# Lending the ring of split weight pairs to expert weights in a two-block model kernel

## Chip, cores and metric

The kernel runs on one core of one Trainium2 chip. Its time is the device time of one execution in microseconds (us), given as the median of several runs. Engine names: PE is TensorE, PEld its weight loads, DVE is VectorE, ACT is ScalarE, POOL is GpSimd, SP is SyncE, whose queue issues nearly all transfers here.

## What is computed

Two blocks follow each other on 256 tokens of width 1024, all in float32. Block 1 is a mixer (pooling and differential attention, closed by the dense product with `w_out`) and then a layer of 32 experts, of which each token takes two. Block 2 is a state-space layer (SSM), a latent-attention layer (MLA) and a last norm. The part around the change, cut to its core:

```python
x = x + (gate_p * pool_out + gate_a * attn_out) @ w_out[l]        # last dense product of block 1
hn = rmsnorm(x, norm2_g[l]).reshape(B * S, D)
x = x + hier_moe(hn, ...)                                          # router, then 32 experts:
#   hdn = silu(xb @ w_gate[e]) * (xb @ w_up[e]);  y = (hdn @ w_down[e]) * wb
...
u = rms_norm(h, norm_w[0])                                         # block 2, first layer
y = ssd_mixer(u, ...)                                              # begins with u @ ssm_in_w
```

The weights of the 32 experts are 32 x 3 x 2 MB = 192 MB. All of them are loaded, whatever the router chooses.

## The kernel before

**Weights come as one list.** `specs` holds every weight piece in the order of use, each 8 KB per partition or less (1 MB in all for a full one). `Weights.issue` (L64) takes the next piece of the list, allots a tile `raw` in some pool, and has SP issue one transfer into it (L77). Pieces of dense layers are worked on further; pieces of experts (192 of them, step `None`) are read by PE as they are.

**Dense pieces are split.** PE works here on pairs of reduced-precision float32 tiles. `_split` (L81) takes 1024 columns of a raw piece: ACT copies them, rounded, into `whi`, and DVE subtracts to get the remainder `wlo` (both L92). Each of the two tiles is 4 KB per partition, and the pool `chp` keeps four of each (`CH_BUFS`): this is the ring of split pairs, 32 KB per partition in all. A product then takes three matmuls per pair: `whi` with the high part of the input, then two more, in `mm3` (L401 to L404) or, as a generator that lets other work in between, `mm3s` (L408). Where the weights are PE's stationary operand (`gemm_feat`, `fine_feat`), the last of the three reads `wlo`; where they are the moving one (`gemm_tok`, `last_out`), it reads `whi`. Splits run ahead of their use by three pairs (five in block 2, where two more pairs live in another pool, `W.more`).

**Where expert weights may lie.** Raw tiles come from four pools: `rawp` (3 slots, L213), `raw2` (7, L778), `raw3` (5, L808) and `raw4` (1, L969), 16 slots of 8 KB. The last three open one after the other as block 1 frees its space. When PE has used a piece, `W.done` (L125) issues the next piece of the list into the pool just freed; with `until=expert_end` these three pools take no piece behind the experts, so the first pieces of the SSM layer go to `rawp` alone. SP issues in the order of the program, and a transfer waits on SP until its slot is free; each also reuses one of eight semaphores, so at most eight are under way.

**The stage between.** The last dense product takes the last four pairs at once (`cs = W.take(4)`, L928) and works through `last_out`; its last use of `whi` are two extra matmuls (`WARM3`, L954). Then come the router (`place`, L856) and the first gather (`gather0`, L917), and then the eight rounds of experts, four experts each: `gate_up` (L1033, matmuls L1043), `hidden_T`, `down` (L1062, matmuls L1069), with the gather of the next round and the scatter of the last one woven in. A round uses 24 pieces. During the eight rounds no pair is split: `W.stop` holds the splits back until L1124, behind the last round.

**Order.** A scheduler places the instructions of each engine when the program is built; a few `order(...)` calls pin pairs of them. So a change of a tile's size or of what it waits for can move instructions elsewhere in the program.

Of the kernel before, what the change touches and what calls it, by code (L numbers as in the profile page):

```python
# [10 lines left out]
F32R = mybir.dt.float32r  # L11
# [7 lines left out]
P = 128  # L19
# [7 lines left out]
CH_BUFS = 4  # L27
MORE = 2
CH = 1024
# [3 lines left out]
HOLD1 = 4  # L33
HOLD2 = 3
ATT = 0.08


class Weights:


    def __init__(self, tc, raw_pool, ch_pool, specs):
        self.tc, self.nc = tc, tc.nc
        self.raw_pool, self.ch_pool = raw_pool, ch_pool
        self.specs = specs
        self.raw = {}
        self.issued = 0
        self.chunks = []
        self.stop = None
        for i, (ap, a, b, step) in enumerate(specs):
            if step is None:  # L50
                self.stop = len(self.chunks)
                continue
            for a0 in range(0, a, step):
                self.chunks.append((i, a0, min(step, a - a0), b, a0 + step >= a))
        self.split = 0
        self.next_whole = None
        self.ready = {}
        self.used = 0
        self.behind = ()
        self.more = None  # L60
        self.between = lambda: None
        self.limit = CH_BUFS + MORE
# [18 lines left out]
    def _split(self):  # L81
        nc = self.nc
        c = self.split
        i, a0, n, b, last = self.chunks[c]
        v = self.raw[i][0][:, a0:a0 + n, :]
        pool = self.more if self.more is not None and c % (CH_BUFS + MORE) >= CH_BUFS else self.ch_pool
        bufs = CH_BUFS if pool is self.ch_pool else MORE
        hi = pool.tile([P, CH], F32R, name="whi", tag="whi", bufs=bufs)
        lo = pool.tile([P, CH], F32R, name="wlo", tag="wlo", bufs=bufs)
        hv = hi[:, :n * b].rearrange("p (a b) -> p a b", b=b)  # L90
        lv = lo[:, :n * b].rearrange("p (a b) -> p a b", b=b)
        pair = self.last = (nc.scalar.copy(hv, v), nc.vector.tensor_sub(lv, v, hv.bitcast(F32)))  # L92
        for later, earlier in zip(pair, self.behind):
            if earlier is not None:
                order(self.tc, later, earlier)
        self.ready[c] = (hv, lv)
        if last:
            _, pool, until = self.raw.pop(i)
            self.issue(pool, until)
        self.split += 1  # L100
# [48 lines left out]
def order(tc, later, earlier):  # L149

    tc.add_manual_dep(later.ins, earlier.ins.name,
                      mybir.DependencyInfo(mybir.DependencyClass.NoSync, mybir.DependencyReason.DATA), reason="order")
# [50 lines left out]
def model_kernel(ctx: ExitStack, tc: tile.TileContext, ap, out, taps=None, stop=None):  # L203
# [10 lines left out]
    ch_pool = ctx.enter_context(tc.tile_pool(name="chp", bufs=CH_BUFS))  # L214
# [23 lines left out]
    for e4 in range(0, 32, 4):  # L238
        for name, step in (("w_expert_gate", 2), ("w_expert_up", 2), ("w_expert_down", 1)):
            kt, n = ap[name].shape[2] // P, ap[name].shape[3]  # L240
# [5 lines left out]
    expert_end = len(specs)  # L246
# [14 lines left out]
    W = Weights(tc, raw_pool, ch_pool, specs)  # L261
# [260 lines left out]
    with b1:  # L522
# [7 lines left out]
        hl = wx.tile([P, 8, T], F32R, name="hl", tag="hl")  # L530
# [303 lines left out]
        def x_part(t, k0, n, add):  # L834

            c = slice(k0 * P, (k0 + n) * P)
            nc.vector.tensor_add(x_sb[:, t, c], x_sb[:, t, c], add)
            sq, sc = rt.tile([P, 512], F32, name="sq")[:, :n * P], ss[:, t, k0 // 2:k0 // 2 + 1]
            if k0 < 6:
                square_sum(x_sb[:, t, c], sq, sc)  # L840
            else:
                nc.vector.tensor_tensor_reduce(sq, x_sb[:, t, c], x_sb[:, t, c], 1.0, 0.0, OP.mult, OP.add, sc)
            if k0 == 0:
                lt[t] = mp.tile([P, 512], F32, name="m")
            ps = mp.tile([P, 4, P], F32, name="m")
            for k in range(n):
                nc.tensor.transpose(ps[:, k], x_sb[:, t, (k0 + k) * P:(k0 + k + 1) * P], ident)
            xT = rt.tile([P, 4, P], F32, name="xT", bufs=2)
            act = nc.scalar.copy(xT[:, :n], ps[:, :n])
            for k in range(k0, k0 + n):  # L850
                pe = nc.tensor.matmul(lt[t][:, :40], xT[:, k - k0], wr[:, k], start=(k == 0), stop=(k == 7))
            return act, pe
# [90 lines left out]
        act, _ = x_part(0, 4, 4, po[0])  # L943
# [16 lines left out]
    with ExitStack() as b2:  # L960
# [3 lines left out]
        yp = b2.enter_context(tc.tile_pool(name="exy", bufs=2, space=PSUM, reuse_waits="tile"))  # L964

        rt_.close()
        x2_sb = ctx.enter_context(tc.tile_pool(name="x2p", bufs=1, reuse_waits="tile")).tile([P, 2, D], F32, name="x2_sb")
        raw4_ = ExitStack()
        raw4 = raw4_.enter_context(tc.tile_pool(name="raw4", bufs=1, reuse_waits="tile"))  # L969
# [437 lines left out]
    with ExitStack() as b4:  # L1407
# [206 lines left out]
        def rest(share):  # L1614

            while share >= ATT * done[0]:
                done[0] += 1
# [161 lines left out]
```

## Time and profile before

| what | value |
|---|---|
| median of 3 runs | 1102.57 us (1102.52 to 1104.97) |
| the profiled execution, its own time | 1104.54 us |
| its span in the trace | 1102.9 us |
| PE, DVE, ACT busy, share of the span | 90%, 45%, 36% |
| moved by the transfers | 293.64 MB, mean 266 GB/s |

The profile shows one execution. Busy shares are means over stages with different limits, so the share of PE says little by itself: a stage is read from its stretch of time, with the rate of the transfers (GB/s) beside the busy time of the engines. A wait is named by the engine and line that waited, and by what ended the wait last. Where the line is that of a helper (L77, L92, L404, L408), it stands for every call of that helper, so the stretch has to tell which one it is.

### The profile page before, as it was taken

The numbers are of one execution on the slowest core, as the hardware profiler recorded it, in microseconds if no ns is written. First come the engines' busy times: TensorE is split into PE (matmuls) and PEld (weight loads), VectorE is DVE, ScalarE is ACT, GpSimd is POOL, SyncE is SP. The second block draws the span as 40 slices with busy tenths as digits, with TensorE's granted clock in tenths as the row PEclk, the third lists the DMA queues.
The fourth block names the chain that finished last, engine by engine and source line by source line (L and its number), as shares of the span: only waits on it lengthen the run. The fifth ranks groups of instructions, "written<-read, shape, count | busy, mean of one in ns | idle before, by whom it ended". The sixth has DMA issues, their size and how long they took to land. (4 is left out here: it accounts for less than half of the span.)

```text
span 1102.9 us, 14835 instructions
## 1 busy us (share of the span) xinstructions
PE 987.2 (90%) x5981; PEld 688.6 (62%) x5981; DVE 492.0 (45%) x1085; ACT 394.1 (36%) x740; POOL 0.2 (0%) x4
## 2 busy tenths in 40 slices
PE   8999998996979687887967679999999999999997
PEld 6899986441414131231411139899998879999985
DVE  8587565120202010100100037679687576467764
ACT  5456542000000000000000036884855555476652
POOL 0000000000000000000000000000000000000000
PEclk9999998999989899989999999999999999999999
DMA  8444895999999999999999966244335446444331
GB/s 297 153 154 153 292 409 187 409 408 410 408 409 409 409 409 409 409 409 410 409 409 409 409 236 229 94 175 140 128 116 177 150 136 219 134 136 123 116 111 39
DMA packets 97096, 293.64 MB, mean 266 GB/s; under 512 B 6912, under 2 KB 12032, under 8 KB 97024
## 3 DMA queue, kind: packets, MB, share of 16 engines
q1 hardware_dynamic: 96736, 292.13, 70.5%
q8 instruction: 48, 0.79, 0.3%
q10 hardware_dynamic: 288, 0.52, 0.1%
q14 instruction: 24, 0.20, 0.1%
HBM read 291.58 MB, written 1.05 MB: 265 GB/s over the span
## 5 line engine op out<-in xcount | busy, mean ns | idle before, releaser
L92 DVE TENSOR_TENSOR wlo<-raw,whi 128x1024 fp32r<-128x1024 f32 (+2 forms) x175 | 202.8, 1170 | 92.4 <-ACT whi L92 91.0
L92 ACT CAST whi<-raw 128x1024 fp32r<-128x1024 f32 (+2 forms) x175 | 175.6, 1011 | 152.8 <-PE acc L403 52.7
L1043 PE MATMUL ea<-raw,xg 128*32 128x512 f32 x1024 | 173.6, 640 | 55.5 <-DMA raw<-in_w_expert_up_dram 50.1
L1043 PEld LDWEIGHTS ea<-raw,xg 128*32 128x32 f32 x1024 | 34.7, 112 | 171.5 <-DMA raw<-in_w_expert_up_dram 100.5
L1069 PE MATMUL yps<-raw,hT 128*32 128x512 f32 x512 | 103.6, 598 | 30.9 <-DMA raw<-in_w_expert_down_dram 25.5
L408 PE MATMUL acc<-u,whi 128*128 128x256 f32 x512 | 96.7, 286 | 0.0
L1069 PEld LDWEIGHTS yps<-raw,hT 128*32 128x32 f32 x512 | 21.9, 109 | 107.0 <-DMA raw<-in_w_expert_down_dram 63.6
L1052 DVE TENSOR_TENSOR hx<-sg,ea 128x512 f32<-128x512 f32 x8 | 5.5, 688 | 185.0 <-PE ea L1043 185.0
L1084 DVE TENSOR_TENSOR x_sb<-x_sb,m 128x512 f32<-128x512 f32 x32 | 22.0, 687 | 144.4 <-PE m L1083 144.4
L408 PEld LDWEIGHTS acc<-u,whi 128*128 128x128 f32 x512 | 79.9, 189 | 1.5
L408 PE MATMUL acc<-u,wlo 128*128 128x256 f32 x256 | 73.2, 286 | 0.0
L908 PEld LDWEIGHTS m<-Sr,x_sb 128*128 128x128 f32 x224 | 55.0, 334 | 8.8 <-issue 8.1
L1060 ACT COPY hT<-m 128x512 f32<-128x512 f32 x8 | 4.7, 586 | 152.9 <-PE m L1058 152.9
L908 PE MATMUL m<-Sr,x_sb 128*128 128x128 f32 x224 | 55.8, 402 | 0.0
L402 PE MATMUL acc<-hh,whi 128*128 128x256 f32 x192 | 55.8, 291 | 0.0
L404 PE MATMUL acc<-hh,wlo 128*128 128x256 f32 x192 | 54.5, 284 | 0.0
L403 PE MATMUL acc<-hl,whi 128*128 128x256 f32 x192 | 54.3, 283 | 0.0
L1074 ACT COPY ysb<-yps 128x512 f32<-128x512 f32 x16 | 9.3, 587 | 125.9 <-PE yps L1069 125.9
L408 PEld LDWEIGHTS acc<-u,wlo 128*128 128x128 f32 x256 | 48.5, 189 | 0.8
L1027 ACT COPY ST<-m 128x256 f32<-128x256 f32 x8 | 3.0, 374 | 108.6 <-PE m L1025 108.6
L408 PE MATMUL bank<-whi,yhl 128*128 128x512 f32 x128 | 41.0, 396 | 0.5 <-ACT zs L1376 0.5
L402 PE MATMUL acc<-u,whi 128*128 128x256 f32 (+1 forms) x136 | 38.6, 284 | 0.0
(409 smaller groups left out, 1902.4 us busy)
## 6 DMA issues: line engine op xcount, KB each, us to landing
raw<-in_w_expert_gate_dram SPq DMA_DIRECT2D x64, 1024.0 KB, 18.5
raw<-in_w_expert_up_dram SPq DMA_DIRECT2D x64, 1024.0 KB, 18.6
raw<-in_w_expert_down_dram SPq DMA_DIRECT2D x64, 1024.0 KB, 18.5
raw<-in_ssm_in_w_dram SPq DMA_DIRECT2D x24, 1024.0 KB, 5.2
raw<-in_w_in_dram SPq DMA_DIRECT2D x15, 1024.0 KB, 5.3
raw<-in_mla_in_w_dram SPq DMA_DIRECT2D x10, 1024.0 KB, 5.1
raw<-in_ssm_out_w_dram SPq DMA_DIRECT2D x8, 1024.0 KB, 5.1
raw<-in_mla_out_w_dram SPq DMA_DIRECT2D x8, 1024.0 KB, 4.8
```

The source lines that it names most:

```text
L92: pair = self.last = (nc.scalar.copy(hv, v), nc.vector.tensor_sub(lv, v, hv.bitcast(F32)))
L402: nc.tensor.matmul(o, ah, bh, start=first, stop=False, skip_group_check=True)
L403: nc.tensor.matmul(o, ah, bl, start=False, stop=False, skip_group_check=True)
L404: nc.tensor.matmul(o, al, bh, start=False, stop=last, skip_group_check=True)
L408: nc.tensor.matmul(o, a, b, start=first and i == 0, stop=last and i == 2, skip_group_check=True)
L908: nc.tensor.matmul(m[:, k], x_sb[:, t, half * 4 + k::8], Sr[q][:, t], start=(t == 0), stop=(t == 1))
L1043: nc.tensor.matmul(ps[quad(j)], x[:, k, quad(j)], ws[j // 2][:, j % 2, kk * 512:kk * 512 + 512], start=(k == 0), stop=(k == 7))
L1052: nc.vector.tensor_mul(hx[q], sg, ps)
L1060: nc.scalar.copy(hT[q].rearrange("p a b -> p (a b)"), m)
L1069: nc.tensor.matmul(y[half][quad(j)], h[:, k, quad(j)], ws[j // 2][:, j % 2, HALF[half]], start=(k == 0), stop=(k == 3))
L1074: nc.scalar.copy(ys[q][:, HALF[half]], y[half])
L1084: nc.vector.tensor_add(x2_sb[:, t, s], (x2_sb if q else x_sb)[:, t, s], m)
```

## The change

The two tiles of a split pair become the two halves of one tile `whl` of 8 KB, so the ring holds four slots of the size of a raw piece. Behind the end of block 1's last product, ahead of the one issue into `raw4`, four expert pieces are issued into these four ring slots. When PE has used a piece that lies in the ring, the next piece goes there, up to piece `expert_end - 24`; the last 24 expert pieces, one round, go to the 16 other slots again. No arithmetic is added or removed.

```diff
+class Ring:
+    def __init__(self, pool, tag, bufs):
+        self.pool, self.args = pool, dict(tag=tag, bufs=bufs)
+    def tile(self, shape, dtype, name, tag):
+        return self.pool.tile(shape, dtype, name=name, **self.args)
...
-        hi = pool.tile([P, CH], F32R, name="whi", tag="whi", bufs=bufs)
-        lo = pool.tile([P, CH], F32R, name="wlo", tag="wlo", bufs=bufs)
-        hv = hi[:, :n * b].rearrange("p (a b) -> p a b", b=b)
-        lv = lo[:, :n * b].rearrange("p (a b) -> p a b", b=b)
+        hl = pool.tile([P, 2 * CH], F32R, name="whl", tag="whl", bufs=bufs)
+        hv = hl[:, :n * b].rearrange("p (a b) -> p a b", b=b)
+        lv = hl[:, CH:CH + n * b].rearrange("p (a b) -> p a b", b=b)
...
         rt_.close()
+        ring = Ring(ch_pool, "whl", CH_BUFS)
+        for _ in range(CH_BUFS):
+            W.issue(ring, expert_end - 24)
         x2_sb = ...
         W.issue(raw4, expert_end)
```

**Place 1, SP, the issues around the end of block 1.** `raw_N` is the tile that takes the piece; behind it stands what the issue waits for (`DMAHW` an earlier transfer's semaphore, `PE` a matmul that read the slot before). Before; the first row is the last issue that waits for a split (`DVE`), the second is the piece for `raw4`, the rest follow PE's use of the first experts:

```order
L77 DMA raw_1852<-in_w_expert_up_dram 128x2x1024 [waits DMAHW0_49,DVE_49]
L77 DMA raw_2066<-in_w_expert_up_dram 128x2x1024 [waits DMAHW1_49,PE_49]
L77 DMA raw_2083<-in_w_expert_down_dram 128x2x1024 [waits DMAHW2_49,PE_49]
L77 DMA raw_2085<-in_w_expert_down_dram 128x2x1024 [waits DMAHW3_49,PE_49]
L77 DMA raw_2105<-in_w_expert_down_dram 128x2x1024 [waits DMAHW4_49,PE_49]
```

and with the change, from the same piece on:

```order
L87 DMA raw_1804<-in_w_expert_up_dram 128x2x1024 [waits DMAHW0_49,DVE_49]
L87 DMA raw_2011<-in_w_expert_up_dram 128x2x1024 [waits DMAHW1_49,PE_49]
L87 DMA raw_2013<-in_w_expert_down_dram 128x2x1024 [waits DMAHW2_49,PE_49]
L87 DMA raw_2015<-in_w_expert_down_dram 128x2x1024 [waits DMAHW3_49,PE_49]
L87 DMA raw_2017<-in_w_expert_down_dram 128x2x1024 [waits DMAHW4_49,PE_49]
L87 DMA raw_2026<-in_w_expert_down_dram 128x2x1024 [waits DMAHW5_49]
L87 DMA raw_2043<-in_w_expert_down_dram 128x2x1024 [waits DMAHW6_49,PE_49]
```

The four tiles from `raw_2011` on are the ring's; `raw_2026` is now `raw4`'s, behind them, and `raw_2043` is the first that waits for an expert matmul (L1043 of before). The waits on PE in the built program are these: the first two ring issues wait for the last matmul on the first and on the second of the four pairs, the third for the last one on the third pair, the fourth for the second of the two `WARM3` matmuls. Before, the piece for `raw4` waits for the last matmul of `last_out`, since that slot lies where an input of the product lay. The order of the pieces is the same, and the number of transfers too.

**Place 2, ACT, the queries of the MLA layer** (casts L92, now L101, are splits; `qraw` and `qn` are evacuations of the query product, `p` is softmax). Before:

```order
L1579 COPY aT<-m 128x384
L92 CAST whi<-raw 128x384
L1539 COPY qraw<-acc 128x256
L1541 COPY qn<-acc 128x512
L1568 ACTIVATE p,l<-p,mx 128x128
L1568 ACTIVATE p,l<-p,mx 128x256
```

and with the change:

```order
L1592 COPY aT<-m 128x384
L1552 COPY qraw<-acc 128x256
L1554 COPY qn<-acc 128x512
L101 CAST whl<-raw 128x384
L1581 ACTIVATE p,l<-p,mx 128x128
L1581 ACTIVATE p,l<-p,mx 128x256
```

The split's cast has moved behind two evacuations. Such exchanges of a split with one to three neighbours stand on ACT and DVE in block 1's attention, in the SSM layer and in the MLA layer; on PE some small matmuls move past products with them. Between the router and the last round of experts PE, DVE and ACT keep their order.

## Rows read from the trace of the kernel before

**Rows 1.** Windows: busy time of each engine, granted clock and rate by stretch (us).

```profile
core 0: us, PE busy (x) PEld busy (x) DVE busy (x) ACT busy (x) POOL busy (x), PEclk, DMA share, GB/s
150.00:172.10 22.10, 21.90 (x126) 18.54 (x125) 10.17 (x29) 7.58 (x15) 0.00 (x0) 1.00 1.03 409
172.10:177.10 5.00, 3.30 (x19) 2.55 (x18) 3.91 (x28) 1.66 (x2) 0.00 (x0) 0.94 0.74 249
177.10:189.00 11.90, 10.89 (x61) 8.36 (x64) 7.59 (x40) 2.15 (x6) 0.00 (x0) 0.74 0.01 2
189.00:191.00 2.00, 2.00 (x22) 0.60 (x18) 0.15 (x1) 0.00 (x0) 0.00 (x0) 1.00 0.82 178
...
280.00:645.00 365.00, 284.05 (x1383) 93.99 (x1382) 33.02 (x70) 15.21 (x28) 0.00 (x0) 0.96 1.03 409
...
663.00:900.00 237.00, 234.97 (x1560) 210.58 (x1559) 174.65 (x332) 154.18 (x307) 0.00 (x0) 1.00 0.45 149
900.00:1080.00 180.00, 180.00 (x1237) 166.52 (x1237) 119.07 (x247) 107.98 (x207) 0.00 (x0) 1.00 0.42 138
```

**Rows 2.** Waits of SP's queue, 158 to 192 us: total, times, longest.

```profile
SPq L77 <- PE ea L1043: 15.2, 1, 15.2
SPq L77 <- PE bank L404: 13.8, 1, 13.8
```

**Rows 3.** Timeline of PE around the end of block 1 (start us, us, ...).

```profile
172.35 0.28 PE L404 MATMUL bank<-whi,ml 128*128 128x256 f32 x1
...
174.56 0.71 PE L954 MATMUL bank<-whi,mh 128*128 128x512 f32 x2
...
185.85 4.07 PE L1043 MATMUL ea<-raw,xg 128*32 128x512 f32 x32
```

**Rows 4.** Page, part 6: the expert issues (count, KB each, median us to landing).

```profile
raw<-in_w_expert_up_dram SPq DMA_DIRECT2D x64, 1024.0 KB, 18.6
```

**Rows 5.** Waits of PE, 186 to 690 us: total, times, longest.

```profile
PE ea L1043 <- DMA raw<-in_w_expert_up_dram: 50.1, 45, 2.7
PE yps L1069 <- DMA raw<-in_w_expert_down_dram: 25.5, 42, 0.7
```

**Rows 6.** Timeline of PE at the end of the expert stage.

```profile
642.57 1.91 PE L1069 MATMUL yps<-raw,hT 128*32 128x512 f32 x8 [0.67 <-DMA raw<-in_w_expert_down_dram]
645.15 1.91 PE L1069 MATMUL yps<-raw,hT 128*32 128x512 f32 x8 [0.67 <-DMA raw<-in_w_expert_down_dram]
...
654.59 3.81 PE L1149 MATMUL acc<-negm,idr 128*128 128x512 f32 x9 [3.65 <-ACTq L1650]
```

**Rows 7.** Groups of instructions by line and shape: the full-size splits.

```profile
L92 DVE TENSOR_TENSOR wlo<-raw,whi 128x1024 fp32r<-128x1024 f32 x156 | 188.7, 1221 | 83.0 <-ACT whi L92 81.7 <-PE acc L403 0.8
...
L92 ACT CAST whi<-raw 128x1024 fp32r<-128x1024 f32 x156 | 163.1, 1052 | 141.6 <-PE acc L403 42.6 <-PE acc L408 38.3 <-PE bank L408 30.5
```

**Rows 8.** Waits of PE, 0 to 186 us: the one on a split.

```profile
PE acc L403 <- DVE wlo L92: 0.8, 1, 0.8
```

**Rows 9.** Chain of waits in the SSM layer, from two stretches (start us, us, what).

```profile
695.56 2.26 PE acc L408 x19
...
760.16 0.29 PE acc L408
760.44 0.17 PE m L1297 x2
760.61 0.29 PE acc L408
```

**Rows 10.** Transfer queues, 172 to 189 us: packets, MB, share of the engines.

```profile
q8 instruction: 1, 0.02, 0.4%
q14 instruction: 2, 0.02, 0.2%
```

**Rows 11.** Timeline of DVE in the router, the same operation twice.

```profile
176.58 0.28 DVE L892 TENSOR_SCALAR Sr<-Sr,rx 128x128 f32<-128x128 f32 x1
...
181.40 0.28 DVE L892 TENSOR_SCALAR Sr<-Sr,rx 128x128 f32<-128x128 f32 x1
```

## What the time was forecast to be, and why

> **What bounds the kernel now.** I read the rate of the transfers by stretch first, then the waits of SP's queue, then those of PE, then the chain of waits behind the experts. The windows [rows 1] show three regimes. From 280 to 645 us the transfers run at 409 GB/s with their engines' share at 1.03, so they are saturated, while PE is busy 284.05 of 365 us: the expert stage is bound by transfers. From 663 to 1080 us it is the other way round, with PE busy 234.97 of 237 us and 180.00 of 180 us at rates of 149 and 138 GB/s: both layers of block 2 are bound by PE. Between block 1 and the experts lies a hole. The rate is 409 GB/s up to 172.1 us, then 249 GB/s for 5 us, 2 GB/s for 11.9 us, and 178 GB/s for 2 us. The reader is to see that the resource that bounds the next 460 us is all but unused here just before.
>
> SP's waits say why [rows 2]. SP waits 13.8 us for the slot of `raw4` (matmul L404) and then 15.2 us for the first expert matmul (L1043). The first ends with the last product at 172.35 + 0.28 = 172.63 us; the second ends when PE, which starts the experts at 185.85 us [rows 3], has done with the first pieces. In between all 16 slots are taken and unread, so but for the piece of `raw4` nothing can be issued.
>
> Is time won in the hole kept? Two things are needed. PE must be able to follow: in the stage it waits 50.1 us for `up` and 25.5 us for `down` pieces [rows 5], 75.6 us in all, so it has room to run 10 us ahead. And the end must hang on the last transfer: the last rounds of matmuls stand 2.58 us apart (642.57, 645.15), each behind a piece just landed [rows 6], and everything after them follows on PE. So a transfer stage that ends earlier moves the rest of the kernel with it.
>
> **The change, part by part.**
>
> *Four more pieces in the hole.* Each is 1024 KB [rows 4], which is 1.049 MB, and at 409 GB/s [rows 1] takes 2.564 us; four take 10.26 us. Does the hole hold them? At 409 GB/s its 18.9 us could carry 7.73 MB. It carries 249 x 5 + 2 x 11.9 + 178 x 2 = 1.62 MB, so 6.1 MB or 14.9 us are free, and four pieces are 4.19 MB. Are they issued in time? The built order shows what each waits for: the first two and the third wait for matmuls on pairs that are finished before the last L404 at 172.35 us, and the fourth for the second extra matmul, which ends at 174.56 + 0.71 = 175.27 us [rows 3]. The first two cover the engines from 172.1 to 177.2 us, the third to 179.8 us; the fourth and the piece for `raw4`, issued behind 175.27 us, come in time to follow without a gap. All five are over at about 172.1 + 5 x 2.564 = 184.9 us, ahead of the first release by an expert matmul, which doesn't move. Moving the `raw4` piece from 172.63 to some 175.3 us costs nothing: five pieces in line hide it, and were all five held until 175.3 us and 2 us more, they would still be through at 190.1 us, inside the hole. Gain: 10.26 us.
>
> *From 191 us on.* The transfers are saturated before with 16 slots; with 20 slots and four pieces more delivered, each issue finds its slot released no later than before. No gain comes in addition, since there is no idle transfer time left to win, and none is lost.
>
> *The last round on 16 slots.* The refill of the ring stops 24 pieces before the end. Before, 16 slots held 409 GB/s to 645 us [rows 1], also where PE lagged behind a gather; the same 16 slots serve the last 24 pieces in the same order, so I take zero. If a bubble came here, it would give back at most what was won, as the ring would then have lent nothing; that is the zero-gain rival below.
>
> *First pieces of the SSM layer.* They go into `rawp`, in the same slots and behind the same expert matmuls as before; they move with the stage. The first splits find a ring that PE last read a round earlier, so nothing waits there.
>
> *One tile per pair.* The cast into a slot must now wait for the last reader of either half. For products with the weights as moving operand the last of the three matmuls read the high half before too: no change. For those with stationary weights it waits one matmul longer. By the code these are 97 of the 175 splits (32 in block 1, 33 in SSM, 32 in MLA). One matmul is 2.26/19 = 0.119 us apart from the next in a plain product, and 0.45 us where other work is woven in (760.16 to 760.61) [rows 9]. What hides it: ACT's full-size casts already stand waiting 141.6 us for PE's releases [rows 7], and yet PE waits for a split only once, 0.8 us [rows 8]; the splits run three to five pairs ahead. I take 0; the upper bound, with every such wait on the path, is 64 x 0.119 + 33 x 0.45 = 22.5 us.
>
> *Exchanged neighbours.* The scheduler moves splits past one to three instructions in block 1, SSM and MLA. The trace of before cannot show the new order. Downward the bound is what PE idles there: 0.8 us [rows 8] and 237 - 234.97 = 2.0 us, together 2.8 us. Upward I allow one pair (1.052 + 1.221 us [rows 7]) on the path in each of SSM and MLA: 4.5 us. I take 0, being nearest to a PE that is busy 99% to 100% of these stages.
>
> *The router beside busy transfers.* The engines now carry data while routing runs. The same DVE operation takes 0.28 us at 176.58 us, when transfers still ran, and 0.28 us at 181.40 us, when they stood [rows 11]. I take 0.
>
> **The sum.** The profiled execution took 1104.54 us, a span of 1102.9 us and 1.6 us around it; less 10.26 us that is 1094.3 us. It lies 1.97 us above the median of the three runs, 1102.57 us, against which the result will be held, so the forecast is 1102.57 - 10.26 = 1092.3 us, 0.93% faster.
>
> A rule speaks for another rate. The Trainium skill, in "DMA: Bandwidth & Descriptors", section "Where 436 GB/s comes from", says that for transfers between HBM and SBUF the HBM side binds at about 358 GB/s per core. By it a piece would take 2.93 us, the four 11.7 us, and the forecast would be 1090.9 us, an estimate by that page. The trace disagrees: 409 GB/s for 365 us [rows 1], and the measurement decides.
>
> **The rivals.**
>
> *A delayed router.* Small instruction transfers share the engines, one of q8 and two of q14 in 172 to 189 us [rows 10], when the engines were mostly idle. If each now stood behind a full piece and an engine waited for it, the experts would start 3 x 2.564 = 7.7 us later, and so would the release that ends the hole: 1092.3 + 7.7 = 1100.0 us, no measurable change. Against it: where the engines are saturated for 365 us [rows 1], PE's long waits name expert pieces [rows 5], and these explain its idle time. Chance 0.03. The Trainium skill, on the same page, section "Queues, rings and completion order", says that an engine takes turns between its queues packet by packet; by that rule a fetch would wait for a packet, not for a piece, and the time would stay at the forecast. No run so far shows it.
>
> *Costly neighbours.* The exchanged order puts a split on PE's path in SSM and MLA: up to 1092.3 + 4.5 = 1096.8 us, still faster. For it: casts have moved behind evacuations in MLA. Against it: the lead of three to five pairs. Chance 0.05.
>
> *The longer release decides* (the other side). The place is ACT's cast into the ring, the price up to 22.5 us, so 1092.3 + 22.5 = 1114.8 us. To end over 0.3% slower than before it must cost 10.26 + 3.3 = 13.6 us, that is 60% of its bound. For it: ACT waits on just these releases. Against it: PE nearly never waits for ACT's result. Chance 0.04.
>
> *It doesn't do what it says.* The ring pieces land early, but the advance is lost before the end, by a bubble when the ring stops being refilled or by PE not following; then 1102.6 us. For it: for the last 24 pieces the ring is not refilled. Against it: the transfers hold 409 GB/s on 16 slots before [rows 1], and PE has 75.6 us of waits to give up. Chance 0.04.
>
> **How the numbers follow.** The forecast has 0.84. Of these cases the forecast and the costly neighbours are faster by over 0.3% (about what a measurement of this kernel can tell from no change): 0.89. The delayed router and the lost advance lie within: 0.07. The longer release alone ends slower: 0.04. The range reaches from 1092.3 - 2.8 = 1089.5 us to the costly neighbours, 1096.8 us; it leaves out the other three cases, 0.11, and some of the tails.
>
> **What would show it.** In the profile of the changed kernel the rate should stay near 409 GB/s to about 185 us, then fall to nothing for some 5 us, and be back at about 190 us. SP's single wait of 13.8 us should break into shorter ones for the four ring slots, the last of them over at 175.3 us, and the one for the first expert matmul (L1043 of before) shrink from 15.2 to about 12.5 us. The transfers should stay saturated, and the matmul that stands at 645.15 us should stand at about 634.9 us. From there to the end the length should be as before within 1 us. The forecast is wrong if the experts' first matmul starts later than 187 us, if the rate dips below 400 GB/s between 195 and 630 us, if the hole reappears elsewhere, or if PE shows new waits for splits of more than 3 us in all.

## The result and the profile after

| | kernel before | with the change |
|---|---|---|
| median | 1103.77 us (1102.52 to 1107.24, 4 runs) | 1092.49 us (1090.57 to 1093.37, 4 runs) |
| ratio, 95% interval | | 0.9892 [0.9868, 0.9916] |
| profiled execution, its span | 1104.54 us, 1102.9 us | 1093.37 us, 1091.7 us |

The change is faster by 1.1% (0.8% to 1.3%). The forecast was 1092.3 us. Five runs of the changed kernel in a later comparison gave 1093.95 us; the median of all nine is 1093.02 us.

First the windows of the changed kernel, in the stretches of [rows 1] as nearly as its shorter time allows (columns as there):

```profile
core 0: us, PE busy (x) PEld busy (x) DVE busy (x) ACT busy (x) POOL busy (x), PEclk, DMA share, GB/s
150.00:172.10 22.10, 21.24 (x124) 17.72 (x122) 9.78 (x33) 6.72 (x16) 0.00 (x0) 1.00 1.03 408
172.10:177.10 5.00, 3.96 (x19) 3.65 (x20) 4.28 (x31) 2.47 (x7) 0.00 (x0) 0.85 1.03 410
177.10:184.90 7.80, 6.79 (x31) 6.11 (x34) 3.95 (x20) 1.28 (x1) 0.00 (x0) 0.72 0.88 353
184.90:189.00 4.10, 4.10 (x38) 1.15 (x34) 2.21 (x11) 0.00 (x0) 0.00 (x0) 0.89 0.17 24
189.00:191.00 2.00, 2.00 (x21) 0.62 (x24) 0.15 (x1) 0.00 (x0) 0.00 (x0) 1.00 0.95 377
...
280.00:634.70 354.70, 268.12 (x1339) 85.12 (x1341) 30.99 (x67) 15.18 (x28) 0.00 (x0) 1.00 1.03 409
652.70:889.70 237.00, 234.98 (x1555) 210.21 (x1555) 174.51 (x331) 153.42 (x306) 0.00 (x0) 1.00 0.44 149
889.70:1069.70 180.00, 180.00 (x1238) 166.66 (x1237) 119.40 (x247) 107.79 (x207) 0.00 (x0) 1.00 0.42 138
```

The hole has shrunk. The rate stays at 410 GB/s where [rows 1] shows 249, and at a mean of 353 GB/s to 184.9 us where it shows 2 (some 410 GB/s to 183 us, falling behind it); what is left of the hole is 4.1 us at 24 GB/s. Behind it the expert stage has the same 409 GB/s, and the two layers of block 2 the same busy PE (234.98 of 237 us, 180.00 of 180 us).

SP's waits, 158 to 192 us, against [rows 2]:

```profile
SPq L87 <- PE ea L1056: 14.0, 3, 12.4
SPq L87 <- PE bank L413: 12.0, 3, 7.0
SPq L87 <- PE m L888: 3.0, 1, 3.0
```

The one wait of 13.8 us for the slot of `raw4` has become shorter ones, the longest 7.0 us, as SP gets a ring slot each time the product has read a pair. The profile puts the 3.0 us down to L888, but the fourth ring issue starts at 173.68 us, just behind the end of the second extra matmul (`WARM3`) at 172.94 + 0.71 = 173.65 us: this is the wait that the built order has. The wait for the first expert matmul has shrunk from 15.2 to 12.4 us.

Now PE's timeline at the same places as [rows 3] and [rows 6]:

```profile
172.94 0.71 PE L963 MATMUL bank<-whl,mh 128*128 128x512 f32 x2
...
184.35 4.35 PE L1056 MATMUL ea<-raw,xg 128*32 128x512 f32 x32
...
631.10 1.91 PE L1082 MATMUL yps<-raw,hT 128*32 128x512 f32 x8 [0.65 <-DMA raw<-in_w_expert_down_dram]
633.65 1.91 PE L1082 MATMUL yps<-raw,hT 128*32 128x512 f32 x8 [0.64 <-DMA raw<-in_w_expert_down_dram]
...
643.10 3.91 PE L1162 MATMUL acc<-negm,idr 128*128 128x512 f32 x9 [3.66 <-ACTq L1663]
```

These rows split the 11.2 us of span. The two extra matmuls (`WARM3`), whose start stands here and below for the last product of block 1, come 174.56 - 172.94 = 1.62 us earlier. From them to the last matmuls of `down` it was 645.15 - 174.56 = 470.59 us and is 633.65 - 172.94 = 460.71 us: 9.88 us from the hole. From there to the end it was 1102.9 - 645.15 = 457.75 us and is 1091.7 - 633.65 = 458.05 us: 0.3 us lost. The sum is 1.62 + 9.88 - 0.30 = 11.2 us. So two causes are to be tested: the hole, which was forecast, and a piece of block 1, which was not. The distance from the last product of block 1 to the last `down` matmuls serves below as the measure of the hole, since what comes before these matmuls doesn't enter it.

PE's waits for experts, 186 to 680 us, are all but those of [rows 5]:

```profile
PE ea L1056 <- DMA raw<-in_w_expert_up_dram: 48.5, 42, 3.0
PE yps L1082 <- DMA raw<-in_w_expert_down_dram: 26.6, 41, 0.7
```

So PE still waits 75.1 us for pieces (75.6 before): the stage is still bound by transfers, and PE has followed the advance.

And the full-size splits, against [rows 7]:

```profile
L101 DVE TENSOR_TENSOR whl<-raw,whl 128x1024 fp32r<-128x1024 f32 x156 | 188.8, 1221 | 74.3 <-ACT whl L101 72.6 <-PE acc L413 0.8
L101 ACT CAST whl<-raw 128x1024 fp32r<-128x1024 f32 x156 | 162.8, 1052 | 122.7 <-PE acc L413 47.4 <-PE acc L417 31.7 <-PE bank L417 30.5
```

ACT stands idle 122.7 us before these casts, less than the 141.6 us before; of that, the three releases by PE that the row names are 109.6 us (111.4 before). One split costs what it cost.

### The profile page after: what moved, and what is told of

Same layout as the page of the kernel before. It is cut to its first block, busy times and chain, and to the rows that moved or that the text cites. A ratio compares the mean times of both kernels' runs of the same rounds, so it can differ in the third digit from the quotient of the medians.

```text
span 1091.7 us, 14807 instructions
## 1 busy us (share of the span) xinstructions
PE 977.3 (90%) x5981; PEld 687.9 (63%) x5981; DVE 492.1 (45%) x1085; ACT 393.7 (36%) x740; POOL 0.2 (0%) x4
## 5 line engine op out<-in xcount | busy, mean ns | idle before, releaser
L101 DVE TENSOR_TENSOR whl<-raw,whl 128x1024 fp32r<-128x1024 f32 (+2 forms) x175 | 202.9, 1171 | 83.5 <-ACT whl L101 81.5
L101 ACT CAST whl<-raw 128x1024 fp32r<-128x1024 f32 (+2 forms) x175 | 175.4, 1012 | 130.1 <-PE acc L413 53.6
L1056 PE MATMUL ea<-raw,xg 128*32 128x512 f32 x1024 | 161.3, 605 | 54.0 <-DMA raw<-in_w_expert_up_dram 48.5
L1056 PEld LDWEIGHTS ea<-raw,xg 128*32 128x32 f32 x1024 | 33.4, 109 | 162.3 <-DMA raw<-in_w_expert_up_dram 93.2
L417 PE MATMUL acc<-u,whl 128*128 128x256 f32 x768 | 103.2, 286 | 0.0
L417 PEld LDWEIGHTS acc<-u,whl 128*128 128x128 f32 x768 | 94.5, 189 | 2.4
L411 PE MATMUL acc<-hh,whl 128*128 128x256 f32 x192 | 55.8, 290 | 0.0
L413 PE MATMUL acc<-hh,whl 128*128 128x256 f32 x192 | 54.7, 285 | 0.0
L412 PE MATMUL acc<-hl,whl 128*128 128x256 f32 x192 | 54.3, 283 | 0.0
L417 PE MATMUL bank<-whl,yhl 128*128 128x512 f32 x192 | 46.0, 395 | 0.4 <-ACT zs L1389 0.4
L417 PE MATMUL bank<-whl,oh 128*128 128x512 f32 x128 | 41.0, 398 | 0.0
L417 PEld LDWEIGHTS bank<-whl,yhl 128*128 128x128 f32 x192 | 35.7, 188 | 8.1 <-ACT zs L1389 0.6
L417 PE MATMUL acc<-whl,u 128*128 128x512 f32 x144 | 40.7, 410 | 0.0
```

The lines of the kernel that those rows point to most:

```text
L411: nc.tensor.matmul(o, ah, bh, start=first, stop=False, skip_group_check=True)
L412: nc.tensor.matmul(o, ah, bl, start=False, stop=False, skip_group_check=True)
L413: nc.tensor.matmul(o, al, bh, start=False, stop=last, skip_group_check=True)
L417: nc.tensor.matmul(o, a, b, start=first and i == 0, stop=last and i == 2, skip_group_check=True)
L1056: nc.tensor.matmul(ps[quad(j)], x[:, k, quad(j)], ws[j // 2][:, j % 2, kk * 512:kk * 512 + 512], start=(k == 0), stop=(k == 7))
```

## The experiments

Two theories were set against rivals. For the hole: every piece delivered in it is 2.56 us that stay to the end, and the four standing slots bring nothing more. For block 1: the merged tile has changed the scheduler's order on ACT, and that removes a stall. Each of these kernels was timed in five rounds against the kernel before. The summary, with the distance just defined from the one profiled execution of each row:

| kernel | median us (runs) | ratio, 95% interval | last product of block 1 | last `down` | distance |
|---|---|---|---|---|---|
| before | 1103.77 (4) | | 174.56 | 645.15 | 470.59 |
| before, again | 1104.59 (11) | 1.0006 [0.9994, 1.0017] | 175.40 | 646.02 | 470.62 |
| merged tile alone | 1102.13 (12) | 0.9976 [0.9963, 0.9989] | 173.09 | 643.66 | 470.57 |
| before, ACT's order pinned | 1102.20 (12) | 0.9979 [0.9967, 0.9991] | 172.57 | 643.00 | 470.43 |
| ring lent after the hole | 1102.41 (12) | 0.9984 [0.9972, 0.9997] | 172.69 | 641.97 | 469.28 |
| two slots | 1097.92 (6) | 0.9946 [0.9930, 0.9962] | 173.07 | 639.88 | 466.81 |
| the change | 1092.49 (4) | 0.9892 [0.9868, 0.9916] | 172.94 | 633.65 | 460.71 |
| the change, again | 1093.95 (5) | 0.9911 [0.9897, 0.9926] | 173.11 | 632.28 | 459.17 |
| ring filled once | 1093.07 (5) | 0.9887 [0.9867, 0.9906] | 173.57 | 633.76 | 460.19 |
| ring never stopped | 1093.26 (5) | 0.9908 [0.9893, 0.9922] | 172.42 | 632.57 | 460.15 |
| old order on ACT | 1093.43 (4) | 0.9910 [0.9893, 0.9926] | 172.69 | 633.37 | 460.68 |
| old order, again | 1093.69 (5) | 0.9906 [0.9886, 0.9927] | 173.26 | 633.09 | 459.83 |
| a fifth piece | 1089.15 (4) | 0.9867 [0.9851, 0.9884] | 173.42 | 629.99 | 456.57 |
| a fifth piece, again | 1091.39 (4) | 0.9885 [0.9868, 0.9902] | 175.28 | 632.71 | 457.43 |

**The change again**, on the chip on which experiments 4 to 6 ran:

> The changed kernel once more, beside the runs of this call. Theory (the hole pays 10.0 us, the order of ACT in block 1 pays 1.5 to 2): 11 to 12 us below the kernel before, last down matmul at about 633.7 us. Rival (part of the first difference was the state of that chip): less than 9 us below.

It came out 9.3 us below the kernel before, 1093.95 against 1103.25 us, less than the theory's 11 to 12 us and a little more than the rival's 9. The intervals of the two comparisons, [0.9868, 0.9916] and [0.9897, 0.9926], overlap. Its trace is on the theory's side: the last `down` matmuls stand at 632.28 us, and its span, 1090.3 us, is the shorter one; but that execution, 1091.98 us, was the fastest of the five.

**1. The merged tile alone.** The change without the loan:

```diff
-        ring = Ring(ch_pool, "whl", CH_BUFS)
-        for _ in range(CH_BUFS):
-            W.issue(ring, expert_end - 24)
```

> One tile per pair is kept, but no piece is issued into the ring. Theory (the hole of 18.9 us between the last product and the experts is filled with four pieces, 10.3 us; the rest of the 11.5 us comes from block 1, where the exchanged neighbours on ACT spare PE a stall at about 40 us and the 1.2 GHz stretch behind it): only block 1's part stays, about 1.5 us under the kernel before, some 1101 us, with the hole of 17 to 19 us back. Rival (the exchanged order in the later layers brings the gain): near 1092.5 us. Rival (the clock stretch comes and goes by chance): no difference from the kernel before, 1102.6 us.

The hole is back, as two windows of this kernel show:

```profile
172.10:177.10 5.00, 3.81 (x19) 3.49 (x19) 4.32 (x31) 2.37 (x7) 0.00 (x0) 0.79 0.64 216
177.10:189.00 11.90, 10.89 (x65) 7.33 (x68) 6.43 (x32) 1.44 (x2) 0.00 (x0) 0.80 0.09 18
```

The distance is 470.57 us, that of the kernel before (470.59). So the hole's gain belongs to the loan and to nothing else. The time is still 0.24% (0.11% to 0.37%) below the kernel before (1104.31 us beside it): block 1's part comes with the merged tile, and the longer release that the merged tile brings costs nothing that shows, although ACT's casts now wait for the last reader of either half.

**2. The ring filled once.** Four pieces in the hole, no refill:

```diff
-            W.issue(ring, expert_end - 24)
+            W.issue(ring, W.issued + 1)
```

> The four ring slots are filled once, at the end of block 1, and never refilled: from the first round on there are 16 slots as before. Theory (the advance is won once, in the hole, and 16 slots are enough to keep the transfers saturated): as the changed kernel, 1092.5 us within 0.7 us, last expert matmuls at about 633.7 us. Rival (20 standing slots are what helps, by covering PE's lag at the gathers): part or all of it is lost, 1095 to 1101 us, with the rate under 400 GB/s somewhere between 200 and 300 us.

The transfers stay saturated on 16 slots for the whole stage, as in the changed kernel:

```profile
280.00:630.00 350.00, 270.54 (x1326) 85.02 (x1325) 31.57 (x71) 15.19 (x28) 0.00 (x0) 0.96 1.03 409
```

The time, 1093.07 us, and the distance, 460.19 us, are the changed kernel's. Four pieces, once, are the whole effect; keeping the ring filled up to `expert_end - 24` brings nothing.

**3. The ring lent after the hole.** The same loop, moved behind the first round of experts, where the hole is over:

```diff
             if q < 7:
                 down(q)
+            if q == 0:
+                ring = Ring(ch_pool, "whl", CH_BUFS)
+                for _ in range(CH_BUFS):
+                    W.issue(ring, expert_end - 24)
```

> The ring is lent only after the first round of experts, so 20 slots stand from then on but the hole is as before. Theory (hole): no gain beyond that of one tile per pair, about 1101 us, rate 409 GB/s from 191 us on with the hole as before. Rival (standing slots): most of the gain, 1093 to 1096 us.

With 20 slots from then on, the last `down` matmuls come at

```profile
641.97 1.91 PE L1079 MATMUL yps<-raw,hT 128*32 128x512 f32 x8 [0.64 <-DMA raw<-in_w_expert_down_dram]
```

and the time is 1102.41 us, that of the merged tile alone (1102.13 us). The distance, 469.28 us, is 1.3 us below that kernel's, while the four executions without a loan lie within 0.2 us of each other. So a gain of about a microsecond from the standing slots isn't excluded, but the time doesn't show it, and it was not followed up. This is the mirror of experiment 2: slots without the hole are worth little or nothing, the hole without standing slots is worth all that the change brings there.

**4. Two slots.** The ring lends two of its four:

```diff
-        for _ in range(CH_BUFS):
+        for _ in range(2):
```

> The ring lends two of its four slots. Theory (each piece of 2.56 us delivered in the hole is kept to the end, nothing else about the ring counts): the hole pays 5.1 us in place of 10.0, block 1's part of 1.5 to 2 us stays, so 6.6 to 7.1 us below the kernel before and 4.9 to 5.1 us above the changed one; the rate of 409 GB/s ends near 178.5 us and the idle stretch is about 5 us longer. Rival (it is the number of standing slots or their place in the list that pays, or PE stops following past a certain advance): the gain is not proportional, within 2 us of the changed kernel or of the kernel with the merged tile alone (1102).

The bytes that the weight queue had moved by 186 us, inside the hole in each kernel (page part 3 for 0 to 186 us: packets, MB, share), first before, then two slots, then the change:

```profile
q1 hardware_dynamic: 19616, 43.99, 66.4%
```

```profile
q1 hardware_dynamic: 20160, 46.09, 68.5%
```

```profile
q1 hardware_dynamic: 20704, 48.19, 72.2%
```

The steps are 2.10 and 4.20 MB, two and four pieces of 1.049 MB: exactly what was lent was delivered, and at 409 GB/s these are 5.1 and 10.3 us. The time is 1097.92 us, 5.3 us below the kernel before and 4.0 us above the changed kernel of the same comparison. That is proportional within the scatter, though short of the expected 6.6 us below and 4.9 us above. The distance, 466.81 us, has gained only 3.8 of the 5.1 us. The missing 1.3 us are of the size by which the distance of one and the same kernel moves (460.71 and 459.17 for the change); more on that in the last section.

**5. The ring never stopped.** The refill runs to the end of the experts:

```diff
-            W.issue(ring, expert_end - 24)
+            W.issue(ring, expert_end)
```

> The ring goes on taking expert pieces to the end of the experts in place of stopping 24 pieces before it. Theory (16 slots serve the last round as well as 20 do, and the first SSM pieces reach rawp in time either way): same as the changed kernel within 1 us, last down matmul within 0.7 us of its place. Rival A (the last round lacked the four slots): faster by up to 2.6 us, with a higher rate in the last 60 us of the experts. Rival B (the first SSM splits now wait for ring slots that the last experts hold): the last down matmul as in the changed kernel, but the rest behind it 1 to 5 us longer, with DVE or ACT waiting for PE in L101 behind 633 us.

The time is 1093.26 us against 1093.95 us of the changed kernel in the same comparison, the distance 460.15 us. Neither rival shows. The last round didn't lack the slots: its last `down` matmuls, 632.57 us, stand between those of the change's two executions. The length from there to the end is 1091.6 - 632.57 = 459.0 us against 458.05 us in the change, just where the second rival begins. But ACT's casts wait no longer for PE there (632 to 700 us: 4.7 us for L417, 4.6 in the change). What differs is the granted clock from 640 to 650 us, 0.66 against 0.83.

**6. A fifth piece.** Some 4 us of the hole are left, and a piece needs 2.56 us. The 8 KB of `x2_sb`, the output of the experts, are first written after the first round; they take an expert piece of that round before.

```diff
-        x2_sb = ctx.enter_context(tc.tile_pool(name="x2p", ...)).tile([P, 2, D], F32, name="x2_sb")
+        x2p = ctx.enter_context(tc.tile_pool(name="x2p", ...))
...
         W.issue(raw4, expert_end)
+        W.issue(Ring(x2p, "x2", 1), W.issued + 1)
...
+            if q == 0:
+                x2_sb = x2p.tile([P, 2, D], F32, name="x2_sb", tag="x2", bufs=1)
```

> One more piece is lent a place in the hole: the 8 KB of x2_sb, which is first written when the first round of experts is done, hold an expert piece of that round before. Theory (the hole still has 4 to 5 us of idle transfers; a piece of 2.56 us fits): 2.56 us below the changed kernel, so about 14 us below the kernel before; the rate of 409 GB/s lasts to about 187 us and the last down matmul stands at about 631.1 us. Rival (the slot is free too late, or the writer of x2_sb waits for the reader of the piece and holds the first scatter up): no gain, or up to 3 us slower than the changed kernel, with a new wait before the first write of x2_sb.

```profile
172.10:177.10 5.00, 3.81 (x19) 3.26 (x20) 4.32 (x32) 2.33 (x6) 0.00 (x0) 0.80 1.02 406
177.10:189.00 11.90, 10.89 (x67) 7.62 (x70) 6.62 (x35) 1.49 (x2) 0.00 (x0) 0.80 0.93 352
...
629.99 1.91 PE L1083 MATMUL yps<-raw,hT 128*32 128x512 f32 x8 [0.68 <-DMA raw<-in_w_expert_down_dram]
```

The hole is all but closed: 352 GB/s from 177.1 to 189 us. The time is 1089.15 us, 14.1 us below the kernel before.

> The kernel with one more piece in the place of x2_sb once more, to fix its size. Theory (one piece of 2.56 us): 13.5 to 14.6 us below the kernel before, last down matmul between 629.5 and 631.5 us. Rival (the 14 us of the first run were in part the restart of the transfers going well once): about 12.5 us below, no more than 1.5 us better than the changed kernel.

The second time it was 1091.39 us, 12.3 us below, as the rival had it, so the first size was partly luck. The last `down` matmuls, at 632.71 us, came later than forecast, because block 1 ended late in this execution (175.28 us). All eight runs of the two have a median of 1089.56 us against 1093.02 us of the change's nine, 3.5 us less; the distances (456.57 and 457.43 us) lie 3.1 us below the mean of the six kernels that lend four slots once or longer (460.12 us). One piece, 2.56 us, is within the scatter of either. This version is faster than both kernels, by some 0.3% against the change.

The profile of the second execution also shows where executions of one kernel differ: it lost some 2 us of block 1 before 20 us, as in two windows of it

```profile
14.00:16.00 2.00, 1.74 (x4) 1.45 (x5) 2.00 (x9) 1.71 (x2) 0.00 (x0) 0.50 1.08 367
16.00:18.00 2.00, 2.00 (x9) 1.81 (x9) 0.58 (x1) 0.35 (x1) 0.00 (x0) 0.50 1.07 349
```

where the granted clock is 0.50 (1.2 GHz); in the first execution it is 1.00 there. PE had waited 1.32 us just before (until 10.76 us), but in the first execution it waited 1.45 us at the same place and kept its clock, so the length of that wait doesn't tell the two apart.

**7. Block 1: ACT's order in the kernel before.** The trace of before has a stall of PE and, behind it, a stretch at the low clock:

```profile
40.91 1.95 PE L598 MATMUL m<-half,sq 128*128 128x2 f32 x16 [0.46 <-ACT sq L591]
...
43.30:46.40 3.10, 3.10 (x9) 2.42 (x8) 2.79 (x11) 0.00 (x0) 0.00 (x0) 0.52 0.04 12
```

PE waits 0.46 us for `sq`, the square of the queries, because ACT does four copies of the keys first. The same two steps of ACT before, and then with the change:

```profile
37.47 2.36 ACT L581 COPY kz<-m 64x512 f32<-64x512 f32 x4
39.84 1.03 ACT L591 ACTIVATE sq<-acc 128x1024 f32<-128x1024 f32 x1
```

```profile
37.33 1.02 ACT L600 ACTIVATE sq<-acc 128x1024 f32<-128x1024 f32 x1 [1.78 <-PE acc L413]
38.25 2.35 ACT L590 COPY kz<-m 64x512 f32<-64x512 f32 x4
```

With the change `sq` comes first, PE doesn't stall, and the clock stays at 1.00. In this experiment the kernel before gets that order and nothing else:

```diff
-                    nc.scalar.copy(kz[s, i, :, t * P:(t + 1) * P], m[s])
+                    kz_copies.append(nc.scalar.copy(kz[s, i, :, t * P:(t + 1) * P], m[s]))
...
-        nc.scalar.activation(sq, ps_q, AF.Square)
+        sq_act = nc.scalar.activation(sq, ps_q, AF.Square)
+        for c in kz_copies:
+            order(tc, c, sq_act)
```

> The kernel before with one thing pinned: on ACT, in block 1, the square of the query product stands ahead of the four copies of the keys, as the changed kernel's order has it; two tiles per pair, no lending. Theory (PE's 0.46 us stall at 40.5 us there pulls the granted clock to 1.2 GHz for about 3 us): 1.5 to 2 us under the kernel before, about 1101 us, clock 1.00 from 40 to 50 us. Rival (the clock stretch comes by chance): no difference, 1102.6 us within 0.7 us.

The time falls by 0.21% (0.09% to 0.33%), the same as with the merged tile alone; block 1's last product stands at 172.57 us, and the granted clock of 40 to 50 us is 1.00 (0.83 before):

```profile
40.00:50.00 10.00, 10.00 (x54) 8.54 (x53) 5.58 (x16) 5.20 (x6) 0.00 (x0) 1.00 0.45 135
```

So in the kernel before this one exchange on ACT is enough to bring block 1's part. That it is also what brings it in the changed kernel doesn't follow; that is the next question.

**8. The reverse.** The changed kernel with the old order pinned, `order(tc, sq_act, c)` in place of `order(tc, c, sq_act)`, the rest as in experiment 7.

> The changed kernel with one order pinned as it stood before: on ACT in block 1 the four copies of kz come ahead of the square of the queries. Theory (this order alone costs a stall of PE of about 0.46 us at 40.5 us and, behind it, some 3 us at a granted clock of 0.50): the stall and the fall of the clock come back at 40 to 47 us, the last matmul of block 1 stands 1.5 to 2 us later than in the changed kernel, near 174.6 us, the hole still pays 10 us, and the time is 1.5 to 2 us above the changed one, about 10 us below the kernel before. Rival (block 1's part came from other exchanged splits): within 0.7 us of the changed kernel, its clock in 40 to 50 us at 1.00.

```profile
40.92 1.95 PE L611 MATMUL m<-half,sq 128*128 128x2 f32 x16 [0.35 <-ACT sq L602]
...
40.00:50.00 10.00, 9.65 (x51) 8.00 (x50) 5.33 (x16) 4.92 (x5) 0.00 (x0) 1.00 0.46 121
```

The stall is back, though 0.35 us and not 0.46, and the clock doesn't fall. Block 1's last product stands at 172.69 us, not near 174.6. The time, 1093.43 us, can't tell: the distance to the changed kernel's nine runs is 0.4 us, and the intervals are wider than the question. So the stall by itself doesn't cost the 1.6 us; most of that is the fall of the clock, which doesn't follow every stall here. And since the old order on ACT doesn't bring the fall back, that order alone isn't what frees the changed kernel of it: something else in it does so too.

**9. Both once more.** Whether the fall in the first trace of before was an event of that one execution was still open.

> The kernel before, unchanged, for a second profiled execution. Open is why the clock fell at 43 to 46 us in the first one. Theory S (the stall of 0.46 us in front of the square's readers makes it fall): PE stalls at 40.5 us again and the granted clock falls to 0.50 within 6 us behind it; time 1102.5 to 1105. Theory E (the fall is an event of single executions, with or without that stall): the stall is there, the clock falls elsewhere in block 1 or not at all; without a fall the last matmul of block 1 stands near 173 us in place of 174.56 and the time is near 1102.

```profile
41.76 1.95 PE L598 MATMUL m<-half,sq 128*128 128x2 f32 x16 [0.46 <-ACT sq L591]
...
40.00:50.00 10.00, 9.54 (x43) 7.72 (x42) 4.29 (x15) 4.67 (x6) 0.00 (x0) 0.83 0.34 107
```

The kernel before shows the same stall of 0.46 us and the same granted clock of 0.83 in this window a second time. Its median also shows how much of a difference is noise: 1104.59 us, against 1102.82 us for 15 other runs of the same kernel beside it, with a ratio that can't be told from 1. The 2 us of block 1 in the medians are hardly more than that; they rest on the intervals and the traces.

> The changed kernel with the old order of ACT in block 1 once more. Theory S: a stall of PE near 40.5 us and the clock at 0.50 for some 3 us behind it this time, 1.5 to 2 us above the changed kernel (about 1094.8). Theory E: the stall without a fall behind it, as in the first look, and a time within 0.7 us of the 1093 us of the changed kernel's runs so far.

The changed kernel with the old order shows 0.35 us and a clock of 1.00 a second time, at 1093.69 us. So neither theory holds as it was put. It hardly is an event of single executions: both traces of the kernel before have the fall between 40 and 50 us, and none of the twelve others has it. Nor does any stall do it, since 0.46 us was followed by the fall in both executions and 0.35 us in neither. The traces show one more difference there: from the eight transposes of the keys (L578, L589) to the stall PE runs 13 products of 128x512 in the kernel before and 14 in the changed kernel with the old order. Which of the two decides, or whether it is something else, was not tried.

## Why the prediction was right, and by how much by luck

**Four more pieces in the hole** (10.26 us): right. The bytes by 186 us are four pieces more, 4.20 MB, and the distance fell from a mean of 470.55 us (four executions without a loan: two of before, the merged tile, the pinned order) to 460.12 us (six with four slots in the hole), by 10.4 us. Its signs came within a microsecond or two: saturated to about 183 us where 185 was forecast, 4.1 us of idle transfers in place of the expected 5, back at 189 to 191 us, L1056's wait 12.4 us where 12.5 was forecast. The rate that was taken from the trace held, 410 GB/s in the hole's first 5 us. The 358 GB/s per core of the Trainium skill ("DMA: Bandwidth & Descriptors", section "Where 436 GB/s comes from") is not the rate of the saturated stretches here, which is 408 to 410 GB/s. The Trainium skill's page "HBM Reference", section "Specifications (TRN2)", says that a core that streams alone gets well above that share; the 409 GB/s here agree with it.

**From 191 us on** and **the last round on 16 slots** (0): right within about a microsecond, by experiments 2, 3 and 5: filled once, lent late or refilled to the very end, the kernels end where the theory of the hole puts them, with the 1.3 us of experiment 3 open.

**The router beside busy transfers** (0): right within 0.3 us. From the last product of block 1 to the first expert matmul it took 185.85 - 174.56 = 11.29 us and takes 184.35 - 172.94 = 11.41 us, now beside transfers at 410 and 353 GB/s. The rival of the delayed router, with 7.7 us, is excluded by that. The Trainium skill, in "DMA: Bandwidth & Descriptors", section "Queues, rings and completion order", says that an engine takes turns between its queues packet by packet. The 0.12 us agree with it, since a whole piece would be 2.56 us.

**One tile per pair** (0, bound 22.5 us): right. Experiment 1 has nothing but the merged tile in it and isn't slower but faster, and ACT's idle time before its casts hasn't grown with the change (122.7 us against 141.6). The rival on the slower side falls. The 141.6 us of [rows 7], which the prediction read as waits for PE's releases, are all of ACT's idle time before these casts; the three releases by PE in that row are 111.4 us of it.

**Exchanged neighbours** (0, bounds -2.8 and +4.5 us): mis-sized. This is the step that failed. It looked for the gain in PE's idle time, and found 0.8 us in block 1 and 2.0 us in block 2; the 0.8 us [rows 8] are only the wait on a split, and the 0.46 us on `sq` weren't in it. Block 2 kept its length within 0.3 us, so the costly neighbours didn't come. The gain was in block 1, 1.62 us in the two profiled executions and 2.1 to 2.2 us in the medians of experiments 1 and 7, and most of it was not idle time: PE was busy in all of 43.3 to 46.4 us, at half its clock. The 40 slices of the page hide it: the slice reads 9 like its neighbours. A window of 40 to 50 us reads 0.83, and the prediction rested on none there. That the gain comes with the merged tile is shown (experiment 1); which of the exchanged neighbours brings it is not, as experiment 8 keeps the clock at 1.00 with ACT's order taken back.

**The reference.** The sum was held against the median of three runs, 1102.57 us; beside the result the kernel before had 1103.77 us, and later between 1102.82 us (15 runs) and 1104.31 us (29 runs). So the forecast came within 0.2 us by luck: the missing gain in block 1 and a reference that was low by 1.2 us cancelled. By the gains alone 10.26 us was forecast and 11.3 us measured.

## What to carry to other kernels

A stage bound by transfers should be entered with as many of them done as will fit: a slot borrowed once, in a stretch where the transfers stand idle for want of slots, is worth its piece's transfer time to the end, and a slot that stands for the whole saturated stage was worth next to nothing here. Count the idle bytes of the hole ahead of it, not the slots. And where a change lets a scheduler choose again, read the granted clock of the stretches around each exchanged pair, not only the idle time there.

## What was not expected of the hardware

A stall of PE of less than half a microsecond was followed by a loss of over three times its length. In the kernel before, 0.46 us at 40.5 and at 41.3 us was followed by a granted clock of 0.50 (1.2 GHz in place of 2.4) for some 3 us, in two executions of two, while 0.35 us at the same place in another program was followed by none, in two of two. What decides between the two the runs don't show. A longer stall is no surer sign: of the two executions of experiment 6 one has a wait of 1.32 us with a fall behind it, the other one of 1.45 us at the same place without. A fall also accounts for most of the one router that was longer than the others: with the ring filled once, the two extra matmuls took 1.20 us at 0.50 against 0.71 us at 1.00, and the experts started 185.59 - 173.57 = 12.02 us behind their start in place of 11.41 us.

The transfers don't restart alike after the hole. Between 186 and 196 us the changed kernel moved 2.61 MB in one execution and 3.13 MB in another (rates of the windows by their lengths), 1.3 us of a saturated stage, though block 1 ended within 0.2 us of the same time. The windows of the two, and then two of 1 us from the first:

```profile
186.00:196.00 10.00, 10.00 (x77) 5.28 (x69) 1.26 (x7) 0.60 (x1) 0.00 (x0) 1.00 0.74 261
186.00:196.00 10.00, 10.00 (x74) 5.47 (x66) 1.56 (x8) 0.60 (x1) 0.00 (x0) 1.00 0.83 313
...
191.00:192.00 1.00, 1.00 (x16) 0.26 (x8) 0.00 (x0) 0.00 (x0) 0.00 (x0) 1.00 0.97 242
192.00:193.00 1.00, 1.00 (x10) 0.49 (x3) 0.00 (x0) 0.32 (x1) 0.00 (x0) 1.00 0.84 311
```

The engines are 97% busy at 242 GB/s there, where a saturated stretch has 409. From 196 us on all kernels run at 409 to 410 GB/s, so this scatter stays to the end of the program. It is most of the 1.5 us between the change's two distances, and of the size that experiment 4 fell short by, though there it was not shown to be the cause. Why a restart goes well or badly the runs don't tell.
